# Seven products for eight in the value and gate projections of two of four blocks

## The chip, the cores and the metric

The kernel runs on one core of one Trainium2 chip. The metric is the device time of one execution in microseconds. In the profile PE is TensorE's matmuls, PEld its weight loads, DVE VectorE, ACT ScalarE, POOL GpSimd and SP SyncE, whose queue issues nearly all DMAs.

## The reference

One decoder layer over 2048 tokens of width 1024, in float32: a mixer of two groups of heads, then a squared-ReLU MLP, each between two RMSNorms.

```python
z = h @ w_in                       # h = rmsnorm(x): 2048 x 1024; w_in: 1024 x 3600
gq, gk, gv, gg, glr, hq, hf, hi, hg = jnp.split(z, _split_points(), axis=-1)
log_a = jax.nn.log_sigmoid(glr @ w_gk_up + b_gk) / 16             # GLA, 4 heads, dk 64, dv 128
o_a = chunked_gated_linear_attention(q_a, k_a, v_a, log_a)
o_a = gated_head_norm(o_a, gg, gla_norm_w)                        # rmsnorm(o) * w * silu(gate)
f = lb + (1 - lb) * jax.nn.sigmoid(hf)                            # HGRN2, 4 heads, df 128, dv 128
o_b = chunked_gated_linear_attention(q_b, 1 - f, v_b, jnp.log(f))
o_b = gated_head_norm(o_b, hg, hgrn_norm_w)
mix = jnp.concatenate([o_a, o_b], axis=-1) @ w_out
h = x + rmsnorm(mix, post_mix_norm)
h = h + rmsnorm(jnp.square(jax.nn.relu(rmsnorm(h, pre_mlp_norm) @ w_up)) @ w_down, post_mlp_norm)
```

The change concerns the columns of `w_in` that make the values (`gv`, `hi`) and the gates of the outputs (`gg`, `hg`).

## The kernel before

Every operand is split into a high part, rounded to fp32r, and the rest (`split`: a copy on ACT makes the high part, a subtraction on DVE or POOL the low one). Each product is three matmuls, high x high, high x low, low x high (`mm3`, L301 to L303, which accumulate in PSUM).

The mixer runs over four blocks `b` of 512 tokens. `hn[b]` holds the normalised input, transposed: 8 tiles `act` of 128 channels by 512 tokens, high and low. A block runs four units in the order `u` = 0, 2, 3, 1; units 0 and 1 are pairs of GLA heads, 2 and 3 of HGRN2 heads. A unit has two parts on TensorE:

- `zchan` makes the q, k or f, q channels, 128 channels by 512 tokens, with the weights as TensorE's stationary operand.
- `values` makes 256 value and 256 gate columns, tokens on partitions. For each of 4 token tiles it multiplies 8 input tiles of 128 tokens with 8 weight pieces of 512 columns, 24 matmuls. Unit 0 has 16 more columns (`glr`) and does 272 and 256 columns in two runs of 24. ACT and DVE evict each tile: a copy, and the sigmoid chain for the gate.

Chunk work (scores, states, transposes, outputs) of a unit runs as generator tasks (`spawn`), of which each `step` emits one piece between the products. After the units `out_proj` multiplies the eight heads' outputs with `w_out` in two halves of 512 columns, and beside it `prepare` makes `hn` of the next block. rstd values (`rs`, L310) are one operation on POOL each.

The weights come in 72 pieces a block: per unit 4 or 8 channel pieces and 8 value pieces, then 16 for `out_proj`, always read in this order. Block 0 loads raw pieces (`in_w_mix` to `wr`, 4 buffers, 256 KB), splits them (ACT and POOL, L291 and L292) and stores the parts in the DRAM tensor `w_split` (L126), as block 1 does for its first 12. From there on pieces of 512 KB are loaded from `w_split` (L114) as soon as one of 12 buffers `w` is freed:

```python
if self.split < i or i >= self.freed + self.LIVE:
    return
z = self.part()
y.nc.sync.dma_start(z[:, :, :n].bitcast(F32), self.store[i % PIECES, :, :, :n])
```

A framework schedules the program onto the engines' queues and puts in the semaphores; on SP the DMAs are issued in queue order, one waiting for its buffer holds back those behind it, and each waits for the one eight places ahead to land. After the mixer come `up` and `down` (the MLP), which already use seven half-size products for eight on operands made and stored beforehand. They are not changed. A second, slower layer with `exact` set follows behind a test of the data; it is not executed here.

Of the kernel before, what the change touches and what calls it, by code (L numbers as in the profile page):

```python
# [27 lines left out]
WM = 528  # L28
# [15 lines left out]
def pieces():  # L44


    out = []
# [16 lines left out]
    return out


class Weights:
# [7 lines left out]
    LATE = 12

    def __init__(self, layer, store):
        self.layer, self.plan, self.raw, self.parts = layer, [], {}, {}
        self.store = store
        self.loaded = self.split = self.taken = self.freed = 0  # L80

    def add(self, n, chan=False, eng="vector"):
        self.plan.append((n, chan, eng))

    def part(self):
        y = self.layer
        return y.wp.tile([P, 2, WS], F32R, tag="w", name=y.name("w"), bufs=self.LIVE)

    def give(self, z):

        n, chan, _ = self.plan[self.split]
        hi, lo = z[:, 0, :n], z[:, 1, :n]
        if chan:
            hi, lo = (x.rearrange("p (k n) -> p k n", n=P) for x in (hi, lo))
        self.parts[self.split] = (hi, lo)
        self.split += 1

    def load(self):
        y = self.layer
        while self.loaded < len(self.plan):  # L100
            i = self.loaded
            n = self.plan[i][0]
            if i < PIECES + self.LATE:
                if i >= self.split + self.RAW:
# [4 lines left out]
                self.raw[i] = raw
            else:  # L110
                if self.split < i or i >= self.freed + self.LIVE:
                    return
# [1 line left out]
                y.nc.sync.dma_start(z[:, :, :n].bitcast(F32), self.store[i % PIECES, :, :, :n])  # L114
# [32 lines left out]
class Layer:
# [1405 lines left out]
```

## Time and profile before

| | |
|---|---|
| runs | 2272.88, 2272.98, 2270.74 us, median 2272.88 |
| profiled execution | 2269.14 us, span 2267.3 us, mean granted TensorE clock 0.995 |
| mixer, four blocks | 0 to 985 us: 250 for block 0, 245 for each other |
| up and down | 985 to 2267 us |
| busy over the span | PE 98%, DVE 62%, ACT 48%, POOL 28% |
| DMA | 428.02 MB, mean 189 GB/s |

The busy times of PE are of instructions whose modelled ends overlap, so the length of a matmul in a stream is read from the distance between starts. PEld runs beside PE.

### The profile page before, as it was taken

What the parts mean: (1) busy time and instruction counts of PE and PEld (TensorE: products, weight loads), DVE (VectorE), ACT (ScalarE), POOL (GpSimd) and SP (SyncE); (2) the same over time, 40 slices, a digit from 0 to 9 for tenths busy, and PEclk for the clock granted to TensorE, in tenths of its full rate; (3) what the DMA queues carried; (4) which work ended last, traced back from release to release, by engine and by line L of the source; (5) the groups of instructions that cost most, each with busy time, mean ns of one, the idle gap of its engine ahead of it and who ended that gap; (6) DMA issues with size and microseconds to landing.
All of it is one profiled execution on the core that took longest, in us unless ns stands there. A gap on an engine that the chain in (4) does not pass through costs nothing.

```text
span 2267.3 us, 30672 instructions
## 1 busy us (share of the span) xinstructions
PE 2216.5 (98%) x10922; PEld 1830.8 (81%) x10922; DVE 1408.5 (62%) x2264; ACT 1089.3 (48%) x2104; POOL 643.5 (28%) x444
## 2 busy tenths in 40 slices
PE   8999999999999999999999999999999999999996
PEld 7788888888888978876888888888778878888884
DVE  6764565343652575377765686656536876777687
ACT  6764565334543554365555565555643322333255
POOL 4444301010100220035522343322322332232344
PEclk9999999999999999999999999999999999999998
DMA  7766974467545974378844474443434433443356
GB/s 244 262 232 241 322 257 149 138 237 281 181 151 176 349 286 158 130 270 281 294 151 152 177 238 163 152 153 144 176 126 135 130 123 110 130 140 117 116 148 132
DMA packets 249810, 428.02 MB, mean 189 GB/s; under 512 B 19872, under 2 KB 93872, under 8 KB 249648
## 3 DMA queue, kind: packets, MB, share of 16 engines
q1 hardware_dynamic: 245520, 418.10, 53.6%
q0 software_dynamic: 3552, 6.82, 1.9%
q8 instruction: 88, 1.44, 0.3%
q10 hardware_dynamic: 576, 1.05, 0.1%
q14 instruction: 74, 0.61, 0.1%
HBM read 289.44 MB, written 136.45 MB: 188 GB/s over the span
## 4 chain that ended last, share of the span: by engine, by line
PE 48%; DVE 2%; DMA 2%; ACT 2%; issue 1%; POOL 1%; SPq 0%; DVEq 0%; ACTq 0%; POOLq 0%
PE Y_f L1057 3%; PE Y_f L1059 3%; PE Y_f L1058 3%; PE Y_f L1358 3%; PE Y_f L1359 3%; PE Y_f L1360 3%; PE X_f L1358 2%; PE X_f L1360 2%; PE X_f L1359 2%; PE Z_f L1059 2%; PE Z_f L1057 2%; PE Z_f L1058 2%; PE Z_f L1360 2%; PE Z_f L1359 2%; PE Z_f L1358 2%; PE X_f L1059 2%
## 5 line engine op out<-in xcount | busy, mean ns | idle before, releaser
L301 PE MATMUL zp_f<-w_f,act_f 128*128 128x512 f32 (+2 forms) x896 | 328.6, 367 | 4.2 <-DVE ct_f L319 3.3
L302 PE MATMUL zp_f<-w_f,act_f 128*128 128x512 f32 (+2 forms) x896 | 325.0, 363 | 0.0
L303 PE MATMUL zp_f<-w_f,act_f 128*128 128x512 f32 (+2 forms) x896 | 323.4, 363 | 0.0
L944 ACT ACTIVATE u_f<-raw_f 128x1024 fp32r<-128x1024 f32 x107 | 113.6, 1061 | 331.9 <-PE Y_f L1359 225.4
L310 POOL TENSOR_TENSOR rs_f<-ms_f,c_neghalf 128x1 f32<-128x1 f32 (+1 forms) x80 | 65.1, 820 | 658.0 <-DVE ms_f L308 657.5
L938 POOL TENSOR_TENSOR u_f<-raw_f,u_f 128x1024 fp32r<-128x1024 f32 x49 | 120.4, 2457 | 305.5 <-ACT u_f L944 304.5
L301 PEld LDWEIGHTS zp_f<-w_f,act_f 128*128 128x128 f32 x896 | 168.6, 188 | 31.3 <-DVE ct_f L319 3.7
L303 PEld LDWEIGHTS zp_f<-w_f,act_f 128*128 128x128 f32 x896 | 168.7, 188 | 25.3 <-issue 0.5
L302 PEld LDWEIGHTS zp_f<-w_f,act_f 128*128 128x128 f32 x896 | 168.9, 189 | 24.3 <-issue 0.5
L301 PE MATMUL zp_f<-act_f,w_f 128*128 128x512 f32 x384 | 151.9, 399 | 7.9 <-ACT act_f L294 7.9
L302 PE MATMUL zp_f<-act_f,w_f 128*128 128x512 f32 x384 | 152.3, 397 | 0.1
L303 PE MATMUL zp_f<-act_f,w_f 128*128 128x512 f32 x384 | 151.9, 395 | 0.0
L1313 DVE TENSOR_TENSOR acc_f<-acc_f,Y_f 128x1024 f32<-128x1024 f32 (+1 forms) x91 | 107.5, 1182 | 64.5 <-PE Y_f L1360 63.2
L1358 PE MATMUL Y_f<-act_f,u_f 128*128 128x512 f32 x368 | 142.3, 390 | 4.8 <-ACT Y_f L1350 2.6
L1359 PE MATMUL Y_f<-act_f,u_f 128*128 128x512 f32 x368 | 143.4, 390 | 0.0
L1360 PE MATMUL Y_f<-act_f,u_f 128*128 128x512 f32 x368 | 142.8, 390 | 0.0
L292 POOL TENSOR_TENSOR w_f<-wr_f,w_f 128x512 fp32r<-128x512 f32 (+1 forms) x76 | 105.3, 1395 | 106.1 <-ACT w_f L291 105.4
L944 ACT ACTIVATE w_f<-t_f 128x512 fp32r<-128x512 f32 x128 | 80.1, 629 | 109.7 <-PE Y_f L1058 56.6
L1059 PE MATMUL X_f<-act_f,w_f 128*128 128x512 f32 x256 | 100.2, 391 | 3.6 <-DVE w_f L941 2.7
L1077 DVE TENSOR_TENSOR ev_f<-Y_f,p_f 128x512 f32<-128x512 f32 x94 | 64.6, 688 | 62.8 <-PE Y_f L1059 62.7
L1313 DVE TENSOR_TENSOR acc_f<-acc_f,Z_f 128x1024 f32<-128x1024 f32 (+1 forms) x62 | 73.2, 1181 | 47.6 <-PE Z_f L1360 47.4
L941 DVE TENSOR_TENSOR w_f<-t_f,w_f 128x512 fp32r<-128x512 f32 x96 | 79.9, 832 | 36.7 <-ACT w_f L944 36.7
(294 smaller groups left out, 5767.0 us busy)
## 6 DMA issues: line engine op xcount, KB each, us to landing
w_f<-w_split SPq DMA_DIRECT2D x188, 512.0 KB, 6.3
raw_f<-u_operands SPq DMA_DIRECT2D x224, 256.0 KB, 3.0
u_operands<-ev_f SPq DMA_DIRECT2D x223, 256.0 KB, 2.1
w_split<-w_f SPq DMA_DIRECT2D x64, 512.0 KB, 5.2
wr_f<-in_w_up SPq DMA_DIRECT2D x62, 512.0 KB, 3.5
wide_f<-in_x SPq DMA_DIRECT2D x32, 512.0 KB, 6.9
wr_f<-in_w_mix SPq DMA_DIRECT2D x64, 256.0 KB, 5.0
wr_f<-in_w_down SPq DMA_DIRECT2D x28, 512.0 KB, 4.8
```

What stands on the lines that cost most here:

```text
L301: mm(out, a[0], b[0], start=i == 0, stop=False)
L302: mm(out, a[0], b[1], start=False, stop=False)
L303: mm(out, a[1], b[0], start=False, stop=i == n - 1)
L938: nc.gpsimd.tensor_tensor(out, a, b, op)
L944: self.nc.scalar.activation(hi, raw, AF.Copy)
L1057: mm(z, whi[:, k, :], hi, start=first and k == 0, stop=False, skip_group_check=more)
L1058: mm(z, whi[:, k, :], lo, start=False, stop=False, skip_group_check=more)
L1059: mm(z, wlo[:, k, :], hi, start=False, stop=end, skip_group_check=more)
L1313: nc.vector.tensor_add(a[:, cols], a[:, cols], z[:, cols])
L1358: mm(zx, hi[:, k, tok], whi, start=not loaded and k == 0, stop=False, skip_group_check=loaded)
L1359: mm(zx, hi[:, k, tok], wlo, start=False, stop=False, skip_group_check=loaded)
L1360: mm(zx, lo[:, k, tok], whi, start=False, stop=k == 1, skip_group_check=loaded)
```

## The change

In blocks 2 and 3 `values7` replaces `values`. The block's left operand (512 tokens x 1024 channels) is cut into 2 x 2 parts, tokens by channels, and the weights into 2 x 2, channels by (value, gate). Seven products of 256 tokens x 512 channels x 256 columns, four of them on sums of weight parts and four on sums of left parts, give the four parts of the result (Winograd's form). Each product accumulates two token tiles: for each of 4 channel tiles and 2 token tiles the three matmuls of a split product, 24 in all, of 256 columns (272 in four of unit 0's products, which carry the `glr` columns).

```diff
+    SEVEN = ((0, "base", 0), (4, "sums", 0), (5, "sums", 2), (1, "base", 1), (6, "sums", 1), (2, "base", 2),
+             (3, "sums", 3))
...
+        for step, (i, _, _) in enumerate(self.SEVEN):
+            self.w.pump(2)
...
+            for j in range(2):
+                whi, wlo = self.w.take()
+                for k in (2 * j, 2 * j + 1):
+                    for m in range(2):
+                        hi, lo = left(i, k, m)
...
+                        for a, b in ((hi, whi), (hi, wlo), (lo, whi)):
+                            mm(zm, a, b[:, k % 2, :n], start=opens and k == 0 and b is whi and a is hi,
+                               stop=k == 3 and a is lo, skip_group_check=not opens)
+                self.w.free()
```

Products add into the same banks (X, Y, Z): the result of product 0 is copied to the second bank, and the 512-wide evictions stand between the products. A unit's value pieces in blocks 2 and 3 are 14 of 512 KB, each used by one product for two channel tiles and freed at once, instead of 8 that stay for all token tiles; a block has 96 pieces instead of 72.

The sums of the weights are made once, in block 1, by a task that begins after unit 0 and is drained before `out_proj`. `rows` is the order of pieces, `stage` gives a buffer `st` (3 of them):

```diff
+    def value_sums(self):
...
+        sub = nc.gpsimd.tensor_sub
+        for u in UNITS:
+            w = width(u)
+            for k in range(4):
+                r = []
+                for row in (k, k + 4):
+                    r.append(self.wp.tile([P, WM], F32, tag="wr", name=self.name("wr"), bufs=Weights.RAW))
+                    nc.sync.dma_start(r[-1][:, :2 * w], io["w_mix"][rows["value", u, row * P], :, :2 * w])
+                yield
...
+                sub(t1, g0, v0[:, :256])
+                sub(t3, g, g0)
+                yield
+                sub(t2, g, t1)
+                sub(t4, v[:, :256], t2)
+                yield
+                for half in range(2):
+                    z = self.sum_parts()
...
+                    self.split(hi, lo, raw[:, half * 512:half * 512 + 512].rearrange("p (k n) -> p k n", n=256),
+                               eng=nc.gpsimd)
+                    for t in range(2):
+                        self.keep_sum(u, half * 2 + t, k, z[:, t * 512:t * 512 + 512], 0, 256)
+                    yield
+                if w > 256:
...
@@ mixer
+                if b == 1 and u == 0:
+                    sums = self.spawn(self.value_sums())
+            if b == 1:
+                self.drain(sums)
             self.out_proj(b)
```

`keep_sum` stores 128 x 512 floats (high and low of one sum) to the DRAM tensor `w_sums`. The left operand's sums for blocks 2 and 3 are made in `prepare`, which now takes the input tiles in pairs (k, k + 4); per pair four operations on DVE and two splits (ACT and POOL), kept in `s` and `st` buffers:

```diff
+        nc.vector.tensor_add(a22, a21, a22)
+        nc.vector.tensor_sub(a21, a11, a21)
+        nc.vector.tensor_sub(a11, a22, a11)
+        nc.vector.tensor_sub(a12, a12, a11)
+        hi, lo = self.sum_slot(), self.sum_slot()
+        for h, z in enumerate((x, y)):
+            cols = slice(h * TB, h * TB + TB)
+            self.split(hi[:, cols], lo[:, cols], z, eng=nc.gpsimd)
```

The buffers `w` go from 12 to 8, and 5 buffers `s` come in; block 0 uses these for 16 of its pieces, block 1 for the sums of weights and blocks 2 and 3 for left sums. A stored piece now has the columns in another order (for each 256 columns high, then low).

```diff
-    LIVE = 12
+    BUFS = {"w": 8, "s": 5}
     RAW = 4
```

`out_proj` takes the pieces of half 0 in the outer loop, with four token tiles in four PSUM banks, and evicts half 0 by DVE instead of ACT; half 1 goes two token tiles at a time.

```diff
+        zs = [self.zp() for _ in range(NCH)]
+        for i in range(KT):
...
+            w = self.w.take()
+            for t in range(NCH):
+                part(zs[t], t, w, i)
+                if i == KT - 1:
+                    evac(zs[t], t, 0)
+            self.w.free()
```

On TensorE, in unit 2 of block 2, the first token tile stood so before (`at` is PSUM of the chunk tasks):

```order
L301 MATMUL zp_f957_5691<-w_f913_5425,act_f817_4821 128x512
L302 MATMUL zp_f957_5691<-w_f913_5425,act_f817_4821 128x512
L721 MATMUL at_f949_5634<-c_ident_61,ct_f844_4985 128x128 x4
L303 MATMUL zp_f957_5691<-w_f913_5425,act_f817_4821 128x512
L301 MATMUL zp_f957_5691<-w_f914_5427,act_f820_4840 128x512
L302 MATMUL zp_f957_5691<-w_f914_5427,act_f820_4840 128x512
```

Now there stand the two token tiles of product 0, and, after product 4, product 5 on left sums:

```order
L806 MATMUL zp_f1163_6709<-w_f1121_6504,act_f903_5153 128x256 x6
L806 MATMUL zp_f1163_6709<-w_f1121_6504,act_f910_5193 128x256 x6
L806 MATMUL zp_f1163_6709<-w_f1132_6548,act_f916_5239 128x256 x6
L806 MATMUL zp_f1163_6709<-w_f1132_6548,act_f926_5293 128x256 x6
...
L806 MATMUL zp_f1168_6746<-w_f1134_6564,st_f912_5216 128x256 x2
L806 MATMUL zp_f1168_6746<-w_f1134_6564,st_f913_5217 128x256
```

A piece of weights serves 12 matmuls of half the width, where it served 12 of the full width over four token tiles.

On SP, in block 1, the first pieces of unit 1 stood before in one row, each waiting for a buffer that TensorE frees:

```order
L114 DMA w_f676_3911<-w_split_74 128x2x512 [waits DMAHW0_49,PE_49]
L114 DMA w_f679_3933<-w_split_74 128x2x512 [waits DMAHW1_49,PE_49]
L114 DMA w_f689_3976<-w_split_74 128x2x512 [waits DMAHW2_49,PE_49]
L114 DMA w_f691_3995<-w_split_74 128x2x512 [waits DMAHW3_49,PE_49]
L114 DMA w_f699_4027<-w_split_74 128x2x512 [waits DMAHW4_49,PE_49]
L114 DMA w_f713_4199<-w_split_74 128x2x512 [waits DMAHW5_49,PE_49]
```

Now the task's raw loads and stores stand between them:

```order
L419 DMA wr_f824_4814<-in_w_mix 128x512 [waits DMAHW0_49,Pool_49]
L419 DMA wr_f828_4831<-in_w_mix 128x512 [waits DMAHW1_49,Pool_49]
L459 DMA w_sums_75<-s_f817_4788 128x512 [waits DMAHW2_49,Pool_49]
L459 DMA w_sums_75<-s_f817_4788 128x512 [waits DMAHW3_49]
L459 DMA w_sums_75<-s_f821_4802 128x512 [waits DMAHW4_49,Pool_49]
L459 DMA w_sums_75<-s_f821_4802 128x512 [waits DMAHW5_49]
L139 DMA w_f746_4329<-w_split_74 128x1024 [waits DMAHW6_49,PE_49]
L419 DMA wr_f829_4833<-in_w_mix 128x512 [waits DMAHW7_49,Pool_49]
L139 DMA w_f747_4331<-w_split_74 128x1024 [waits DMAHW0_49,PE_49]
```

The weight loads (L139 after the change) stand behind stores that wait for POOL.

On POOL, in the later units of block 1, rstd rows stood alone before:

```order
L310 TENSOR_TENSOR rs_f694_4013<-ms_f693_4011,c_neghalf_65 128x1 [waits DVE_49,Pool_49]
L310 TENSOR_TENSOR rs_f733_4297<-ms_f732_4295,c_neghalf_65 128x4 [waits DVE_49]
L310 TENSOR_TENSOR rs_f738_4316<-ms_f737_4314,c_neghalf_65 128x4 [waits DVE_49]
L310 TENSOR_TENSOR rs_f785_4639<-ms_f784_4637,c_neghalf_65 128x4 [waits DVE_49,Pool_49]
L310 TENSOR_TENSOR rs_f790_4658<-ms_f789_4656,c_neghalf_65 128x4 [waits DVE_49,Pool_49]
```

Now they stand among the task's subtractions (L424 to L428, and L319 of `split`):

```order
L424 TENSOR_TENSOR st_f835_4854<-wr_f833_4850 128x256 [waits DMAHW3_49]
L337 TENSOR_TENSOR rs_f770_4441<-ms_f769_4439,c_neghalf_65 128x4 [waits DVE_49]
L337 TENSOR_TENSOR rs_f775_4460<-ms_f774_4458,c_neghalf_65 128x4 [waits DVE_49]
L425 TENSOR_TENSOR st_f835_4854<-wr_f834_4852,wr_f833_4850 128x256 [waits DMAHW4_49]
L427 TENSOR_TENSOR st_f835_4854<-wr_f834_4852,st_f835_4854 128x256 [waits Pool_49]
L424 TENSOR_TENSOR st_f840_4873<-wr_f838_4869 128x256 [waits DMAHW5_49]
L428 TENSOR_TENSOR st_f835_4854<-wr_f834_4852,st_f835_4854 128x256 [waits Pool_49]
L319 TENSOR_TENSOR s_f836_4859<-st_f835_4854,s_f836_4859 128x2x256 [waits DMAHW6_49,DMAHW1_49,Activation_49]
```

The rstd rows of unit 3's heads (L337 now) are moved behind subtractions that wait for raw loads and for stores of earlier sums.

More of the change, by code (lines that the diff above doesn't have):

```diff
@@ L27 @@
 NG = FF // P // GF
-WM = 528
+WM = 544
 WS = 576
@@ L49, in chan @@
     def chan(*cols):
-        out.extend(("chan", half * 512, [(col, P)]) for half in range(2) for col in cols)
+        out.extend(("chan", u, half * 512, [(col, P)]) for half in range(2) for col in cols)
     for u in UNITS:
@@ L67 @@
 class Weights:
-    LIVE = 12
+    BUFS = {"w": 8, "s": 5}
     RAW = 4
[L75 to L96, printed above, removed]
+    def __init__(self, layer):
+        self.layer, self.plan, self.pending, self.parts = layer, [], [], {}
+        self.loaded = self.taken = self.freed = 0
+        self.live = {"w": 0, "s": 0}
+    def room(self, i):
+        tag = self.plan[i].tag
+        return self.live[tag] < self.BUFS[tag]
@@ L136, in take @@
     def take(self):
-        if self.split == self.taken:
-            assert self.split - self.freed < self.LIVE
+        self.load()
+        while self.taken not in self.parts:
             self.prep()
@@ L143, in free @@
     def free(self, n=1):
-        self.freed += n
+        for _ in range(n):
+            self.live[self.plan[self.freed].tag] -= 1
+            self.freed += 1
 class Layer:
@@ new lines, in sum_parts, with keep_sum @@
+    def sum_parts(self):
+        return self.wp.tile([P, D], F32R, tag="s", name=self.name("s"), bufs=Weights.BUFS["s"])
+    def keep_sum(self, u, which, k, z, col, n):
+        w = width(u) if which > 1 else 256
+        at = self.wparts["sums"][u, which, k // 2, :, k % 2 * 2 * w:k % 2 * 2 * w + 2 * w]
+        if n == w:
+            self.nc.sync.dma_start(at, z.bitcast(F32))
+        else:
+            self.nc.sync.dma_start(at.rearrange("p (a n) -> p a n", a=2)[:, :, col:col + n],
+                                   z.bitcast(F32).rearrange("p (a n) -> p a n", a=2))
@@ L333, in mixer @@
     def mixer(self):
-        for tag, n, width in (("wr", Weights.RAW, WM), ("w", Weights.LIVE, 2 * WS), ("pad", 1, 48)):
-            self.wp.tile([P, width], F32R if tag == "w" else F32, tag=tag, name=self.name(tag), bufs=n)
+        for tag, n, cols in (("wr", Weights.RAW, WM), ("w", Weights.BUFS["w"], 2 * WS), ("s", Weights.BUFS["s"], D),
+                             ("pad", 1, 48)):
+            self.wp.tile([P, cols], F32R if tag in ("w", "s") else F32, tag=tag, name=self.name(tag), bufs=n)
@@ new lines, in out_proj @@
+            w = self.w.take()
[4 more added lines that the diff above has]
+            self.w.free()
+            self.step()
+            if i in (1, 4):
+                self.step()
+        n = 2 if b + 1 < NBLK else 1
+        w = []
+        for t0 in range(0, NCH, n):
+            zs = [self.zp() for _ in range(n)]
+            for i in range(KT):
+                if i % (4 // n) == 0:
+                    self.w.pump(2)
+                if t0 == 0:
+                    w.append(self.w.take())
+                for t in range(n):
+                    part(zs[t], t0 + t, w[i], i)
+                if t0 + n == NCH:
+                    self.w.free()
+                if i * n % 4 == 3 or i * n % 4 == 2 and n == 2:
+                    self.step()
+            for t in range(n):
+                evac(zs[t], t0 + t, 1)
@@ L1478, in build @@
         c["verdict"] = cp.tile([1, 1], I32, name="c_verdict")
-        wsplit = dp.tile([PIECES, P, 2, WM], F32, name="w_split")
+        wd = {"split": dp.tile([PIECES, P, 2 * WM], F32, name="w_split"),
+              "sums": dp.tile([len(UNITS), 4, 2, P, 2 * WM], F32, name="w_sums")}
         h2d = dp.tile([D, T], F32, name="h2_scratch")
```

345 lines of the change are left out of this document (249 added, 96 removed).

## The prediction

> **What bounds the kernel now.** I read the page's busy shares first, then the busy time of each engine by block, then TensorE's waits.
>
> ```profile
> span 2267.3 us, 30672 instructions
> PE 2216.5 (98%) x10922; PEld 1830.8 (81%) x10922; DVE 1408.5 (62%) x2264; ACT 1089.3 (48%) x2104; POOL 643.5 (28%) x444
> ```
> ```profile
> 250.00:495.00 245.00, 245.00 (x1386) 205.03 (x1386) 124.32 (x325) 115.66 (x290) 23.66 (x24) 1.00 0.62 213
> 495.00:740.00 245.00, 245.00 (x1386) 205.03 (x1386) 117.28 (x320) 111.58 (x282) 16.48 (x20) 1.00 0.59 201
> 740.00:985.00 245.00, 245.00 (x1383) 204.72 (x1382) 129.41 (x318) 118.10 (x292) 38.08 (x34) 1.00 0.66 233
> ```
> The three windows are mixer blocks 1, 2 and 3 (columns: stretch, length, PE, PEld, DVE, ACT, POOL, granted clock, DMA share, GB/s). TensorE is busy for all of each 245.0 us at a granted clock of 1.00; the two longest waits of the run lie in block 0:
>
> ```profile
> PE zp_f L301 <- ACT act_f L294: 7.9, 1, 7.9
> PE zp_f L301 <- DVE ct_f L319: 3.3, 1, 3.3
> ```
> So a block's time is the sum of its matmuls, and matmuls taken out are worth their spacing as long as weights arrive. The spacing is the distance of starts, since the durations overlap:
>
> ```profile
> 876.10 0.39 PE L301 MATMUL zp_f<-w_f,act_f 128*128 128x512 f32 x1
> ...
> 892.19 0.40 PE L303 MATMUL zp_f<-w_f,act_f 128*128 128x512 f32 x1
> ```
> ```profile
> 519.69 0.28 PE L302 MATMUL zp_f<-w_f,act_f 128*128 128x256 f32 x1
> ...
> 522.28 0.28 PE L303 MATMUL zp_f<-w_f,act_f 128*128 128x256 f32 x1
> ...
> 522.66 0.28 PE L303 MATMUL zp_f<-w_f,act_f 128*128 128x272 f32 x1
> ...
> 525.29 0.29 PE L303 MATMUL zp_f<-w_f,act_f 128*128 128x272 f32 x1
> ```
> 16.09 us over 71 gaps is 0.2266 us at 512 columns, 2.59 over 22 is 0.1177 at 256, 2.63 over 21 is 0.1252 at 272.
>
> **Blocks 2 and 3: products.** Per block, units 2, 3 and 1 each lose 96 matmuls of 512 columns (21.75 us) and unit 0 loses 96 of 272 and 96 of 256 (23.32 us). Each unit gains 168 half-width ones: 19.77 us, or for unit 0, where four of seven products keep 272 columns, 96 x 0.1252 + 72 x 0.1177 = 20.49 us. That saves 1.98 us in three units and 2.83 in one, 8.77 a block and **17.5 us** in both. The halved width leaves more weight loads in the same time:
>
> ```profile
> L302 PEld LDWEIGHTS zp_f<-w_f,act_f 128*128 128x128 f32 x62 | 11.7, 188 | 0.0
> ```
> A load takes 188 ns, yet the 256-wide rows, with a load for each matmul, run at 117.7 ns: loads overlap there, so I price them at nothing. The other bound is that spacing becomes 188 ns, a rival below. [...]
>
> **Blocks 2 and 3: other engines.** A unit's evictions were four of ACT's 256-wide copies and sigmoid chains per token tile; they become 512-wide.
>
> ```profile
> L538 ACT ACTIVATE wide_f<-zp_f 128x256 f32<-128x256 f32 x60 | 22.8, 380 | 97.0 <-PE zp_f L303 95.3 <-issue 1.5
> L317 ACT ACTIVATE wide_f<-wide_f 128x256 f32<-128x256 f32 x64 | 26.8, 418 | 1.2
> L786 ACT ACTIVATE ct_f<-zp_f 128x512 f32<-128x512 f32 x32 | 19.0, 596 | 0.0
> L291 ACT ACTIVATE w_f<-wr_f 128x512 fp32r<-128x512 f32 x68 | 41.9, 629 | 45.4 <-DMA wr_f<-in_w_mix 30.5 <-POOL w_f L292 8.3 <-issue 5.0
> L547 DVE TENSOR_TENSOR wide_f<-zp_f,wide_f 128x256 f32<-128x256 f32 x60 | 25.4, 423 | 18.6 <-ACT wide_f L320 18.3
> ```
> ACT goes from about 4 x (2 x 0.38 + 3 x 0.418) = 8.1 us to 5 x 0.596 + 8 x 0.629 = 8.0 us a unit, within 20 us of products: nothing. The token sums of the left operand (prepare) add per block 16 DVE operations of 0.42 (6.8 us), 8 ACT copies of 0.63 (5.0) and 8 POOL subtractions of 1.36 (10.9), beside the output projection of the block before:
>
> ```profile
> 476.00:505.00 29.00, 29.00 (x133) 24.15 (x132) 15.00 (x26) 13.91 (x32) 2.98 (x3) 1.00 0.80 287
> 505.00:567.00 62.00, 62.00 (x378) 54.84 (x377) 26.02 (x63) 29.57 (x61) 3.30 (x5) 1.00 0.81 287
> 750.00:812.00 62.00, 62.00 (x378) 54.79 (x378) 32.99 (x62) 35.27 (x71) 14.29 (x13) 1.00 1.00 355
> ```
> In the first window DVE would stand at 21.8, ACT at 18.9 and POOL at 13.9 of 29 us, and the products that read them (4, 5, 6, 2) stand behind unit 0's channel products, 48 x 0.2266 = 10.9 us: nothing. Moving half 0's eviction from ACT to DVE is off the path too. Weights are not free: a unit loads 14 pieces of 512 KB instead of 8, one for 12 matmuls, 1.41 us. The third window (start of block 3) already moves 355 GB/s at DMA share 1.00, where a piece takes 1.48 us. Eight buffers are 11 us of stock. Bounds for both blocks' starts and streaming: 0, and 10 us (two units at 1.48 for 1.41 and a late first piece in each block); I take **1.2**, near the low end, because the saturated window is one unit of four.
>
> **Block 1: the task.** Per unit and row pair it issues on SP 2 loads and 4 stores of 262 KB, on POOL 4 subtractions of 256 columns and 2 of 512, on ACT 2 copies.
>
> ```profile
> L938 POOL TENSOR_TENSOR u_f<-raw_f,u_f 128x1024 fp32r<-128x1024 f32 x49 | 120.4, 2457 | 305.5 <-ACT u_f L944 304.5 <-DMA raw_f<-u_operands 0.7
> L292 POOL TENSOR_TENSOR w_f<-wr_f,w_f 128x512 fp32r<-128x512 f32 x68 | 92.0, 1363 | 101.9 <-ACT w_f L291 101.4 <-PE zp_f L301 0.2
> L938 POOL TENSOR_TENSOR act_f<-ct_f,act_f 128x512 fp32r<-128x512 f32 x1 | 2.4, 2359 | 1.4 <-ACT act_f L944 1.4
> L310 POOL TENSOR_TENSOR rs_f<-ms_f,c_neghalf 128x4 f32<-128x4 f32 x32 | 32.3, 1010 | 473.4 <-DVE ms_f L308 473.1
> 297.00:453.00 156.00, 156.00 (x878) 127.87 (x877) 82.93 (x244) 76.22 (x195) 8.19 (x10) 1.00 0.52 177
> DMA packets 15190, 27.57 MB, mean 177 GB/s; under 512 B 866, under 2 KB 2914, under 8 KB 15178
> ```
> From 1.363 at 512 and 2.457 at 1024 a 256-wide subtraction is estimated at 0.82 us, so a step takes POOL 4 x 0.82 + 2 x 1.363 = 6.0 us, 16 steps 96 us, and ACT 32 x 0.63 = 20 us. The last two rows are the stretch from unit 0's end to the output projection: 156 us in which POOL works 8.2, ACT 76.2 and DVE 82.9. Unit 0's 16 extra columns add 3 small operations in 4 steps, 12 us at the rstd row's 1.0. With those and the 8.2 POOL would be busy 116 of 156. DMA moves 27.6 MB there; 25.2 more make 52.8, or 338 GB/s, 95% of the 355 above. So it fits, at small margin. Matmuls of block 1 don't read the sums; what can reach them is SP's queue, in which a store that waits for POOL stands ahead of the next weight load, and the heads' rstd behind subtractions on POOL (1.0 us each; I take **0.7** for those, bounds 0 and 6, one step).
>
> **Block 1: eight buffers for twelve.** A unit's values hold all eight pieces until its last token tile. Before, the next unit's first pieces came in four spare buffers:
>
> ```profile
> SPq L114 <- PE zp_f L303: 376.3, 103, 23.4
> w_f<-w_split SPq DMA_DIRECT2D x50, 512.0 KB, 5.9
> DMA to landing us min/median/max: 3.5/6.5/10.0
> ```
> SP stood ready and waited 376 us for TensorE to free buffers. Now the first one comes free, in unit 0, after 3 of the last 24 matmuls, 21 x 0.1177 = 2.5 us before the end (0.8 us of transposes follow), and in the others 21 x 0.2266 = 4.8 us. The load needs 3.5 to 10.0 us. Unit 0 to 2: 0.2 to 6.7, I take **1.5**, since the queue is short there. Unit 2 to 3: 0 to 5.2, **0.4**. Unit 3 to 1 and 1 to output projection: 0 to 5.2 each, plus up to eight 262 KB transfers in flight (5.9 us at 355 GB/s); **2.0** and **1.5**, nearer the median landing (6.5 - 4.8 = 1.7). Later pieces are used at 2.7 us each and catch up. Block 0 has 13 buffers for 12: nothing, bounds -1 and 1.
>
> **Sum.** -17.5 + 1.2 + 0.7 + 1.5 + 0.4 + 2.0 + 1.5 = -10.2. The profiled execution took 2269.1 (span 2267.3 and 1.8 around it), so it would take 2258.9; the median of the runs, 2272.9, lies 3.8 above it, and gives **2262.7**.
>
> **Rivals.** (1) Full gain: the next unit's loads land in time after all, stalls below 3 us; 2255 to 2258. For it: the block-1 window's DMA share of 0.52, and the minimum landing of 3.5. Against: the order of SP's queue.
> (2) Queue backlog: three of the boundaries in block 1 meet a queue full of stores (3 to 5.9 us each) and streaming costs 2 to 4, together 11 to 21.7; 2266 to 2277. For it: 338 of 355 GB/s.
> (3) The other side, POOL's pace: the task must be drained before block 1's output projection, so at p us a step TensorE, through SP's stores, waits 16p + 20 - 156. From p = 8.5 it costs; with the other terms it ends above 2277.4 from 9.4. At 10 it gives 24 us: 2287. For it: the single 2.359 row beside 1.363, and DVE's 82.9 busy us; if each of six operations first waits out one DVE operation of 0.42 to 0.7, p is 8.5 to 10.2. Against: the means over 49 and 68 are taken beside a busy DVE too. [...]
> (4) Weight loads of 188 ns set the spacing: 168 x 0.188 = 31.6 us a unit, 9.8 more than before and 79 in eight: about 2358. Against: the 22 gaps of 117.7 ns. [...]
>
> **Chances.** Forecast (stalls 3 to 11, 2258 to 2266) 0.50, full gain 0.18, backlog 0.18, POOL's pace 0.12, weight loads 0.02. 0.2% of 2272.9 is 4.5 us, about what runs of this kernel can tell from nothing: faster is below 2268.3, slower above 2277.4. Faster takes the first two and a quarter of the third, 0.72; slower the last two, 0.14; same the rest, 0.14. The range, 2254 to 2277, holds the first three; the forecast alone 2258 to 2266.
>
> **What the profile after would show.** Right: blocks 2 and 3 about 236 us long each with half-width matmuls at 0.118 and no idle; in block 1, POOL about 116 us busy between unit 0 and the output projection, steps of 6 us, and TensorE idle for 1 to 2 us at the starts of units, released by weight DMAs. Wrong: a gap of 10 us or more ahead of block 1's output projection, with 256-wide POOL subtractions well over 1.1 us (rival 3); spacing above 0.13 (rival 4); waits for weights spread through blocks 2 and 3 (the streaming term was too small); or idle time at block starts behind the left sums, which I priced at nothing.

## The result and the profile after

The changed kernel takes 2290.07 us (median of 4 runs, 2285.14 to 2294.07), the kernel before 2271.81 in the same comparison: a ratio of 1.008, 95% interval 1.0059 to 1.0101. It is slower by 18 us; 2262.7 was forecast, in a range that ended at 2277. The profiled execution took 2285.14. From the page of the changed kernel, and its windows by block, cut at the first matmul of each block (columns as before: PE, PEld, DVE, ACT, POOL, clock, DMA share, GB/s):

```profile
span 2283.3 us, 31913 instructions
PE 2214.2 (97%) x11306; PEld 1848.4 (81%) x11306; DVE 1466.4 (64%) x2294; ACT 1105.3 (48%) x2092; POOL 772.2 (34%) x572
```
```profile
259.60:519.70 260.10, 251.08 (x1387) 208.05 (x1386) 156.07 (x333) 129.15 (x323) 127.15 (x140) 0.99 0.84 299
519.70:758.40 238.70, 237.69 (x1579) 209.65 (x1578) 133.13 (x332) 117.37 (x265) 29.16 (x27) 1.00 0.76 261
758.40:1008.50 250.10, 242.66 (x1570) 213.14 (x1570) 138.08 (x316) 115.66 (x265) 49.42 (x42) 0.98 0.80 280
```
Cut in the same way, the kernel before took 245.2, 245.3 and 244.1 us for these blocks. So block 2 gains 6.6 us, block 1 loses 14.9 and block 3 loses 6.0: the sum, 14.3, is nearly all of the 16.0 us between the spans. In block 2 TensorE is idle for 1.0 us, in block 1 for 9.0 and in block 3 for 7.4. The waits of TensorE in three stretches, block 1's unit 0 (255 to 300 us), the end of unit 3 and the start of unit 1 in block 1 (400 to 460), block 3's first 90 us (758 to 850):

```profile
PE zp_f L329 <- POOL w_f L319: 2.9, 2, 1.6
```
```profile
PE at_f L1003 <- DVE ct_f L947: 2.1, 1, 2.1
PE zp_f L328 <- DMA w_f<-w_split: 1.7, 1, 1.7
PE at_f L993 <- DVE ct_f L948: 1.2, 1, 1.2
```
```profile
PE zp_f L806 <- DVE ct_f L346: 3.6, 1, 3.6
PE at_f L1154 <- DVE wide_f L1148: 2.2, 1, 2.2
PE zp_f L806 <- ACT zp_f L812: 1.1, 1, 1.1
```
Most of them are waits for VectorE or POOL; only 1.7 us in these stretches are for a weight load. The half-width matmuls themselves run as forecast, here 24 of product 0 in unit 3 of block 2 and what follows them:

```profile
642.37 3.04 PE L806 MATMUL zp_f<-w_f,act_f 128*128 128x256 f32 x24
645.24 0.60 PE L1003 MATMUL at_f<-c_ident,ct_f 128*128 128x128 f32 x4
```
2.87 us from start to start for 24 is 0.1196 us each, against 0.1177: 1.3 us more over a block's 672, and no sign of the 0.188 of the weight loads.

**The granted clock.** A wait costs more than itself. The first row is a window of block 1 with the POOL waits, the second of block 3 behind the 3.6 us; the other three cut block 3's start, where the wait of 2.2 us ends at 771.73, into pieces of 3.41 us:

```profile
270.70:281.00 10.30, 7.30 (x44) 6.66 (x43) 2.96 (x2) 5.36 (x10) 8.82 (x8) 0.83 0.99 350
826.00:833.00 7.00, 7.00 (x76) 6.66 (x74) 6.97 (x22) 5.17 (x12) 0.00 (x0) 0.76 1.05 345
768.27:771.68 3.41, 1.21 (x6) 0.67 (x4) 2.96 (x7) 3.21 (x9) 2.53 (x4) 1.00 0.98 272
771.68:775.09 3.41, 3.36 (x15) 3.36 (x16) 3.31 (x2) 0.58 (x2) 3.41 (x4) 0.50 1.05 417
775.09:778.50 3.41, 3.41 (x30) 3.41 (x29) 2.71 (x5) 2.31 (x5) 3.07 (x3) 1.00 0.81 321
```
In the second TensorE is busy throughout, at 0.76 of its clock. The last three show what this mean is made of: after 3.41 us with 2.20 us of idle time the clock is at half for the next 3.41 us. Block 1 has two such stretches, block 3 three; each costs about 1.7 us. With them block 3 adds up: 244.1 before, less the 7.5 us that the products save (8.77 less 1.3), plus 7.4 of idle time and 5.1 of slow clock, is 249.1 of the 250.1 measured. In block 1, 9.0 of idle time and 3.4 of slow clock leave 2.5 of the 14.9 us unexplained.

### The profile page after: what moved, and what is told of

Read it like the earlier page. It is cut to its first block, busy times and chain, and to the rows that moved or that the text cites. A ratio compares the mean times of both kernels' runs of the same rounds, so it can differ in the third digit from the quotient of the medians.

```text
span 2283.3 us, 31913 instructions
## 1 busy us (share of the span) xinstructions
PE 2214.2 (97%) x11306; PEld 1848.4 (81%) x11306; DVE 1466.4 (64%) x2294; ACT 1105.3 (48%) x2092; POOL 772.2 (34%) x572
## 4 chain that ended last, share of the span: by engine, by line
PE 47%; DMA 2%; DVE 2%; issue 1%; ACT 1%; POOL 1%; SPq 0%; DVEq 0%; ACTq 0%; POOLq 0%
PE Y_f L1338 3%; PE Y_f L1340 3%; PE Y_f L1339 3%; PE Y_f L1639 3%; PE Y_f L1640 3%; PE Y_f L1641 3%; PE X_f L1639 2%; PE X_f L1641 2%; PE X_f L1640 2%; PE Z_f L1639 2%; PE Z_f L1640 2%; PE Z_f L1641 2%; PE X_f L1339 2%; PE X_f L1340 2%; PE X_f L1338 2%; PE Z_f L1340 2%
## 5 line engine op out<-in xcount | busy, mean ns | idle before, releaser
L337 POOL TENSOR_TENSOR rs_f<-ms_f,c_neghalf 128x1 f32<-128x1 f32 (+1 forms) x80 | 64.9, 820 | 473.7 <-DVE ms_f L335 473.5
L329 PE MATMUL zp_f<-w_f,act_f 128*128 128x512 f32 (+2 forms) x548 | 202.8, 371 | 3.0 <-POOL w_f L319 2.9
L328 PE MATMUL zp_f<-w_f,act_f 128*128 128x512 f32 (+2 forms) x548 | 203.3, 375 | 1.1 <-ACT ct_f L723 1.1
L330 PE MATMUL zp_f<-w_f,act_f 128*128 128x512 f32 (+2 forms) x548 | 200.7, 369 | 0.0
L328 PE MATMUL zp_f<-act_f,w_f 128*128 128x512 f32 x328 | 130.6, 398 | 2.5 <-DMA w_f<-w_split 2.5
L330 PE MATMUL zp_f<-act_f,w_f 128*128 128x512 f32 x328 | 129.9, 396 | 0.0
L329 PE MATMUL zp_f<-act_f,w_f 128*128 128x512 f32 x328 | 129.0, 393 | 0.0
L329 PEld LDWEIGHTS zp_f<-w_f,act_f 128*128 128x128 f32 x548 | 104.4, 191 | 19.7 <-POOL w_f L319 3.6
L328 PEld LDWEIGHTS zp_f<-w_f,act_f 128*128 128x128 f32 x548 | 103.5, 190 | 19.0 <-issue 1.4
L330 PEld LDWEIGHTS zp_f<-w_f,act_f 128*128 128x128 f32 x548 | 104.2, 190 | 16.7 <-issue 0.3
L319 POOL TENSOR_TENSOR w_f<-wr_f,w_f 128x512 fp32r<-128x512 f32 (+1 forms) x59 | 84.7, 1450 | 74.1 <-ACT w_f L318 63.4
L1219 POOL TENSOR_TENSOR ev_f<-ev_f,ev_f 128x512 f32<-128x512 f32 x40 | 63.0, 1575 | 124.3 <-ACT ev_f L1362 64.1
```

Source lines behind the costliest of these rows:

```text
L328: mm(out, a[0], b[0], start=i == 0, stop=False)
L329: mm(out, a[0], b[1], start=False, stop=False)
L330: mm(out, a[1], b[0], start=False, stop=i == n - 1)
L1219: nc.gpsimd.tensor_tensor(out, a, b, op)
```

## The experiments

Times of a block or unit are between the first channel matmuls (zchan) in the profiled execution; "rest of block 1" is from unit 2 to the end of the block. Each ratio is to runs of the kernel before in the same comparison (medians 2270.8 to 2271.8). The unchanged down stage took 615 to 622 us from its first to its last matmul in these executions, so the spans of single ones say less than the blocks. Blocks vary too where their code is the same: block 1 by 3 us (e9 and e11), its rest by 4 us (e13 and e14, of which 12.5 and 3.4 us stood at half clock), block 3 from 246.6 to 250.5 (the changed kernel, e1, e2, e3, e5, e6). So a difference of a few us in one block counts only where the medians bear it out.

| | median us | ratio to before (95%) | block 1 | rest of block 1 | block 2 | block 3 |
|---|---|---|---|---|---|---|
| before | 2271.8 | | 245.2 | 208.4 | 245.3 | 244.1 |
| after | 2290.1 | 1.0059-1.0101 | 260.1 | 216.4 | 238.7 | 250.1 |
| e1 odd pieces on DVE | 2289.3 | 1.0064-1.0100 | 261.9 | 217.9 | 238.0 | 250.5 |
| e2 buffers s in unit 0 | 2284.5 | 1.0047-1.0073 | 257.0 | 215.0 | 238.7 | 248.9 |
| e3 no task | 2277.8 | 1.0021-1.0041 | 251.8 | 208.4 | 237.9 | 250.4 |
| e4 no left sums in block 3 | 2285.0 | 1.0048-1.0079 | 261.6 | 217.0 | 238.4 | 247.0 |
| e5 task without arithmetic | 2281.0 | 1.0026-1.0053 | 257.0 | 211.1 | 238.2 | 246.6 |
| e6 task without stores | 2288.7 | 1.0063-1.0090 | 258.7 | 216.3 | 239.3 | 247.5 |
| e7 late combine | 2278.5 | 1.0022-1.0044 | 260.3 | 216.7 | 238.1 | 242.0 |
| e8 seven products in block 2 only | 2291.2 | 1.0075-1.0102 | 261.6 | 217.0 | 238.9 | 251.0 |
| e9 = e2 + e7 | 2277.1 | 1.0018-1.0041 | 258.2 | 214.9 | 238.5 | 239.0 |
| e10 = e9, task on DVE | 2273.2 | 0.9997-1.0017 | 254.8 | 211.5 | 238.5 | 239.9 |
| e11 = e9, left sums on DVE | 2274.0 | 0.9999-1.0017 | 261.3 | 217.6 | 237.3 | 238.4 |
| e12 before with 8 buffers | 2298.1 | 1.0106-1.0139 | 248.2 | 208.1 | 251.2 | 250.6 |
| e13 = all mends | 2269.4 | 0.9976-0.9995 | 256.7 | 214.5 | 237.3 | 238.3 |
| e13 without the task | 2262.3 | 0.9940-0.9966 | 248.0 | 208.1 | 237.3 | 239.5 |
| e14 = e13 + e1 | 2269.6 | 0.9980-0.9997 | 251.9 | 210.5 | 237.3 | 237.6 |

**e1 and e2: unit 0 of block 1.** From its first value matmul to unit 2's first channel matmul it took 32.5 us, 25.6 before (the two texts say 33.1 and 25.8).

```diff
-                    if b == 0 and i < self.LATE and i % 2 and kind == "value":          # e1
+                    if i < self.LATE and i % 2 and kind == "value":
-                if b == 0 and (i < 4 or 12 <= i < 16 or 16 < i < 56 and i % 3 == 2):    # e2
+                if b == 1 and i < 4 or b == 0 and (i < 4 or 12 <= i < 16 or ...):
```


> The changed kernel, but the odd ones of unit 0's eight value pieces in block 1 are split by DVE again, as before the change (there all eight are split by POOL). Theory POOL-splits: unit 0's values in block 1, which took 33.1 us against 25.8 before, return to 26 to 27.5 us and the whole gains 5 to 7 us (2290 to about 2284). Theory eight-buffers: the pieces are late because only 8 buffers w are there; values stay above 31.5 us and the whole within 2 us of 2290.

> The changed kernel, but unit 0's four channel pieces in block 1 go to buffers s (free at that time), so that all eight w are free for its value pieces. Theory eight-buffers: unit 0's values in block 1 fall from 33.1 to below 28 us, the whole gains 4 to 7 us. Theory POOL-splits: the pieces are still split one after the other on POOL; values stay above 31 us and the whole within 2 us of 2290.

e1 changed nothing (32.8 us): who splits does not matter. In e2 both waits for POOL's `w_f` are gone, and the last value matmul stands 26 us after the first, as before the change. So the pieces could not be split ahead while eight `w` also held the channels' pieces. But unit 0 as a whole only went from 43.7 to 41.9 us (30.7 from the first value matmul to unit 2, in place of the "below 28" of the expectation), and the whole's gain of 5.6 us isn't clear of noise, since the intervals overlap: low-rank matmuls of the gate, which stood inside unit 2, now stand ahead of it and wait. Timeline of TensorE in e2, and its windows there:

```profile
299.42 0.73 PE L328 MATMUL at_f<-ct_f,wgk_f 16*128 16x512 f32 x2 [1.06 <-ACT ct_f L318]
...
302.54 0.63 PE L330 MATMUL zp_f<-act_f,w_f 128*128 128x512 f32 x1
302.97 0.63 PE L328 MATMUL zp_f<-act_f,w_f 128*128 128x512 f32 x1
```
```profile
299.07:302.48 3.41, 3.06 (x11) 2.00 (x12) 2.18 (x4) 2.54 (x6) 0.37 (x2) 1.00 1.02 360
302.48:305.89 3.41, 3.41 (x9) 2.65 (x8) 0.69 (x1) 0.43 (x1) 0.00 (x0) 0.50 1.03 423
```
3 us after a wait of 1.06 us the spacing of 512-wide matmuls is 0.43 us, about twice the 0.2266, for 3.41 us. The 3.41 us ahead hold only 0.35 us of idle time, and the six low-rank matmuls (16*128, where the others are 128*128); whether these have a part in it no run shows. In e10 TensorE is idle for 1.06 us in 297 to 359 us too, and the clock stayed at 1.00 there; in e13, with a wait of 1.1 us on the same operation, 302.1 to 320 us stand at 0.84.

**e3, e5, e6: the task, its DMAs, its arithmetic.** e3 drops the spawn and drain; e5 stores the raw tiles; e6 returns from `keep_sum` at once.

```diff
-                    self.split(hi, lo, raw[...], eng=nc.gpsimd)                          # e5, and the four sub()
-                        self.keep_sum(u, half * 2 + t, k, z[:, t * 512:t * 512 + 512], 0, 256)
+                        self.keep_sum(u, half * 2 + t, k, r[half][:, :512], 0, 256)
```


> The changed kernel without the task in block 1: no sums of weights are made, and blocks 2 and 3 load pieces of the same size from w_split in their place (the value products are computed with these). Theory queue-and-POOL (the task's loads, stores and subtractions delay the weight loads and the other engines): block 1 from unit 2 to its end falls from 216.4 us to 208 to 210 (before: 208.4), the whole gains 6 to 9 us. Theory eight-buffers: the boundaries wait for freed buffers whether the task runs or not; 213 to 217 us, the whole gains under 3.

> The changed kernel, but the task in block 1 leaves out its arithmetic: it loads the raw pieces and stores them as they are in the places of the sums (same DMAs, nothing on POOL, ACT or DVE). Theory lock (POOL's subtractions hold up VectorE's operations with two SBUF inputs, VectorE falls behind and TensorE waits for it): block 1 from unit 2 to its end falls from 216.4 us to 208 to 210.5, as without the task (208.4). Theory queue (the stores and loads stand ahead of weight loads on SP and take DMA time): it stays at 213 to 217.

> The changed kernel, but the task makes the sums and doesn't store them (its raw loads stay; blocks 2 and 3 load pieces of the same size from w_split in their place). Theory lock: block 1 from unit 2 to its end stays at 213 to 217 us, with TensorE waiting for VectorE near the end of unit 3. Theory queue: with 64 stores of 256 KB gone from SP's queue it falls to 208 to 210.5 us, and no wait of TensorE on w_split is left.

Without the task the rest of block 1 takes 208.4 us, exactly as before: eight buffers cost nothing at those three boundaries. The DMAs alone (e5) cost 2.7 us, between its two expectations, and 1.7 of them are slow clock behind the waits ahead of unit 2 (TensorE is idle for none of the 211.1 us). The arithmetic with its raw loads (e6) costs 7.9, all together 8.0. The medians agree: leaving out the arithmetic gains 9.1 us, leaving out the stores 1.4. So it is the arithmetic. Yet POOL is not late by its own pace; its operations in the changed kernel (255 to 520 us):

```profile
L319 POOL TENSOR_TENSOR s_f<-st_f,s_f 128x512 fp32r<-128x512 f32 x32 | 42.4, 1331 | 13.2 <-ACT s_f L318 10.7 <-DMA w_f<-w_split 2.2
L425 POOL TENSOR_TENSOR st_f<-wr_f,wr_f 128x256 f32<-128x256 f32 x16 | 13.5, 847 | 9.4 <-DMA wr_f<-in_w_mix 9.4
L427 POOL TENSOR_TENSOR st_f<-wr_f,st_f 128x256 f32<-128x256 f32 x16 | 13.0, 812 | 0.0
L424 POOL TENSOR_TENSOR st_f<-wr_f 128x256 f32<-128x256 f32 x16 | 12.8, 801 | 8.9 <-DMA wr_f<-in_w_mix 8.9
L428 POOL TENSOR_TENSOR st_f<-wr_f,st_f 128x256 f32<-128x256 f32 x16 | 12.5, 779 | 0.4
```
A step is 0.847 + 0.812 + 0.801 + 0.779 + 2 x 1.331 = 5.9 us, as priced (6.0). VectorE is slowed. Its scans in the log decay, in 303 to 440 us of the kernel before, of the changed one, and of e5:

```profile
L643 DVE TENSOR_TENSOR_SCAN ct_f<-c_ones,ct_f 128x128 f32<-128x128 f32 x24 | 8.3, 405 | 0.1
```
```profile
L925 DVE TENSOR_TENSOR_SCAN ct_f<-c_ones,ct_f 128x128 f32<-128x128 f32 x21 | 12.1, 629 | 0.0
```
```profile
L906 DVE TENSOR_TENSOR_SCAN ct_f<-c_ones,ct_f 128x128 f32<-128x128 f32 x24 | 8.3, 406 | 0.1
```
The same instruction takes 405 ns, 629 beside POOL's subtractions, 406 when these are left out (with the task's copies on ACT) and the DMAs stay. Not every operation is stretched; in the changed kernel, the first with both operands in SBUF, the second with one in PSUM (`zp`):

```profile
L948 DVE TENSOR_TENSOR ct_f<-ct_f,ct_f 128x512 f32<-128x512 f32 x5 | 4.8, 968 | 0.0
L346 DVE SCALAR_TENSOR_TENSOR ct_f<-zp_f,ct_f 128x512 f32<-128x512 f32 x8 | 5.3, 677 | 0.4 <-ACT ct_f L345 0.4
```
Before they took 682 and 678 ns. One operation with a single operand in SBUF was stretched too (564 ns for 424). All of VectorE in those 137 us, for e3 and the changed kernel:

```profile
303.00:440.00 137.00, 136.83 (x758) 112.31 (x759) 78.77 (x233) 68.99 (x176) 8.34 (x11) 1.00 0.54 188
```
```profile
303.00:440.00 137.00, 132.77 (x727) 108.66 (x728) 93.53 (x221) 76.14 (x196) 70.01 (x86) 0.99 0.83 296
```
78.8 us of work become 93.5 with fewer instructions. In the changed kernel 3.3 of the 5.1 us that TensorE is idle in the rest of block 1 are waits for VectorE. e6 shows a second path: its longest wait is 3.5 us for `w_split`, at 423.8, without a single store in the queue. There the raw loads, which wait for POOL to free `wr`, stand ahead of the weight loads on SP:

```profile
396.49 23.14 SPq L420 DMA_DIRECT2D wr_f<-in_w_mix  x8
419.69 1.37 SPq L139 DMA_DIRECT2D w_f<-w_split  x3
```
That expectation's "no wait on w_split" fell with the queue theory, and "waiting for VectorE" held for 1.4 us only.

**e4, e7, e8: block 3.**

```diff
-        later = x if b > 1 else None                                                     # e4, e8
+        later = x if b == 2 else None
-                self.spawn(self.combine(0, halves))
             for u in UNITS:
+                if u == 3 and b == NBLK - 1:                                             # e7
+                    self.spawn(self.combine(0, halves))
```


> The changed kernel without the left operand's sums of block 3 (four products there use tiles of the input unsummed): 16 DVE operations, 8 ACT copies and 8 POOL subtractions less beside the output projection of block 2; products, weights and DMA of block 3 stay. Theory left-sums (DVE and POOL, which also build the MLP's first operands there, fall behind): block 3 falls from 250.1 us to 239 to 242 and the whole gains 8 to 11 us. Theory DMA (the 24 pieces more saturate the queue in block 3's first 90 us): block 3 stays above 247 us, the whole within 3 us of 2290.

> The changed kernel, but in block 3 the task that makes the MLP's first left operands (combine: loads of 256 KB, 16 POOL operations, 28 stores) is spawned ahead of unit 3 instead of at the block's start. Theory crowding (block 3's first 90 us hold the left sums, 24 pieces more and this task; POOL and the queue are late and VectorE is held up): the stall of 3.7 us ahead of unit 2's values and the wait at the block's start go, block 3 falls from 250.1 to 238 to 243 us and the whole gains 6 to 12 us. Theory late glr (unit 0's low-rank columns are complete only with the last of seven products, and the gate chain stands ahead of unit 2's sigmoids on ACT and DVE): the 3.7 us stay, block 3 stays above 247.

> The changed kernel with seven products in block 2 alone; block 3 does eight on pieces of w_split, without left sums (buffers, the output projection's order and the task in block 1 stay). Theory seven-in-3 (block 3's loss comes with its pieces, sums and late glr): block 3 returns to 243 to 246 us, and the whole gains 4 to 7 us on 2290. Theory common parts (eight buffers, evictions on DVE): block 3 stays at 249 or more with eight products more of time, 255 or above, and the whole loses.

`combine` is a task of the kernel before, unchanged, which makes operands of the MLP at the start of block 3 (POOL additions L1189 to L1200). With the left sums' subtractions it keeps POOL busy for all of 758 to 769 us. VectorE's operations there read (and below them POOL's subtractions of 755 to 775 us):

```profile
759.27 2.31 DVE L1141 SCALAR_TENSOR_TENSOR wide_f<-wide_f,rs_f,post_f 128x1024 f32<-128x1024 f32 x1 [1.70 <-POOL rs_f L337]
761.50 1.51 DVE L597 TENSOR_TENSOR ct_f<-ct_f,ct_f 128x256 f32<-128x256 f32 x1
762.93 1.51 DVE L595 TENSOR_TENSOR ct_f<-ct_f,ct_f 128x256 f32<-128x256 f32 x1
```
```profile
L319 POOL TENSOR_TENSOR s_f<-ct_f,s_f 128x512 fp32r<-128x512 f32 x4 | 8.2, 2059 | 0.0
```
The first takes 1.27 us in the kernel before at block 3's start (`752.14 1.27`), the others 0.42 where POOL is quiet (e11). Here POOL is slowed as well, 2.06 us for what took 1.33 in the task. TensorE waits there for L1148, behind them. The larger stall, 3.6 us ahead of unit 2's values, is a chain of the gate of unit 0 standing ahead of unit 2's sigmoid on VectorE; timeline of DVE, and of PE with the low-rank matmuls that start this chain:

```profile
821.73 2.40 DVE L925 TENSOR_TENSOR_SCAN ct_f<-c_ones,ct_f 128x128 f32<-128x128 f32 x4
...
824.92 0.69 DVE L346 SCALAR_TENSOR_TENSOR ct_f<-zp_f,ct_f 128x512 f32<-128x512 f32 x1
```
```profile
815.98 0.73 PE L328 MATMUL at_f<-ct_f,wgk_f 16*128 16x512 f32 x2
...
825.66 4.50 PE L806 MATMUL zp_f<-w_f,act_f 128*128 128x256 f32 x23 [3.56 <-DVE ct_f L346]
```
With `combine` moved (e7) both waits go, block 3 takes 242.0 us and the whole 11.6 less. In e7 the low-rank matmuls stand elsewhere too:

```profile
808.09 0.73 PE L328 MATMUL at_f<-ct_f,wgk_f 16*128 16x512 f32 x2
```
Unit 2 begins at 795.66 in the changed kernel and at 792.38 in e7, so they come 20.3 and 15.7 us into it: behind 83 of its 96 channel matmuls and behind 61 (34 in the kernel before; in block 2 of the changed kernel, which has no such wait, 61). In the changed kernel and in e1 to e6, which have seven products and `combine` at the block's start, they stand behind 83; in e7, e9, e10, e11 and e13 behind 61. So e7 doesn't tell crowding on POOL from this order, and the theory of the late low-rank columns had hold of the larger wait, though it expected it to stay.

Without left sums (e4) the wait at the block's start goes: unit 0 takes 34.2 us there, 35.9 to 37.2 in the six executions with the same block 3. The larger stays at 3.6, and block 3 as a whole, 247.0, is not outside what those six show. e4's expectation, either all or nothing, missed. Since unit 0 takes 34.4 us in e7, with left sums and without `combine`, the 2 to 3 us at the block's start come from the two together.

In e8 eight products in block 3 bring 251.0 instead of 243 to 246: the 3.6 us stall is gone, but units 0 and 2 together take 106.2 us (99.2 before), with waits for weights and for the gate's low-rank products between them. So neither theory held as put. Eight pieces held in 8 buffers are a possible reason, which e8 does not show by itself.

**e9, e10, e11: the mends.**

```diff
-        sub = nc.gpsimd.tensor_sub                                                       # e10, in value_sums
+        sub = nc.vector.tensor_sub
-            self.split(hi[:, cols], lo[:, cols], z, eng=nc.gpsimd)                       # e11, in sums_of
+            self.split(hi[:, cols], lo[:, cols], z)
```


> The changed kernel with two of the mends at once: unit 0's channel pieces of block 1 in buffers s, and combine spawned ahead of unit 3 in block 3. Theory (eight buffers in block 1's unit 0, crowding in block 3, both independent): the gains of the single runs add up, 2290 - 5.6 - 11.6 = 2273, 2270 to 2277; block 1 about 257 us, block 3 about 242. Rival (a wait moved away returns later, since POOL still makes block 1's end late and the queue is no shorter): 2278 or more.

> As the last one, but the task's four 256-wide subtractions per step run on DVE instead of POOL (64 x 0.42 = 27 us more on DVE, 52 less on POOL). [...] Rival VectorE-bound (it is busy 93.5 of 137 us there already): no gain, or up to 8 us lost.

> As e9, but the low parts of the left operand's sums (8 subtractions of 512 a block) are made on DVE instead of POOL. Theory lock: at the starts of blocks 2 and 3 DVE's operations return to their lengths (0.42 for 256-wide ones, which took 1.51 us at block 3's start), block 3 and 2 gain 1 to 3 us each. Rival: with combine gone from there POOL no longer holds them up; within 1.5 us of e9.

e9 stands between its two expectations (2277.1), though block 3 fell to 239.0: e2's gain did not add up in block 1. In e10 the whole gains 3.9 us on e9, where the rival had no gain, and the intervals don't overlap; the rest of block 1 falls from 214.9 to 211.5, and scans from 560 to 449 ns. But this doesn't settle how. VectorE's own 64 subtractions take 0.52 to 0.66 us each, and its busy time in 303 to 440 us rises from 88.0 to 103.2. What TensorE no longer waits for are weights; its waits in the rest of block 1, in e9 and in e10:

```profile
PE zp_f L328 <- DMA w_f<-w_split: 3.8, 2, 3.4
```
```profile
PE zp_f L328 <- DMA w_f<-w_split: 0.6, 1, 0.6
```
So e10 fits the second path, raw loads that no longer wait for POOL, at least as well as a VectorE that POOL slows less. e11 brings all VectorE operations of block 3's start back (1.29 and 0.42 us, against 1.92 and up to 0.79 in e9; its rows for the 1024-wide one and a 256-wide one):

```profile
L1142 DVE SCALAR_TENSOR_TENSOR wide_f<-wide_f,rs_f,post_f 128x1024 f32<-128x1024 f32 x3 | 3.9, 1286 | 0.6 <-POOL rs_f L337 0.4
...
L596 DVE TENSOR_TENSOR ct_f<-ct_f,ct_f 128x256 f32<-128x256 f32 x4 | 1.7, 418 | 0.0
```
Block 2 gains 1.2 us on e9 and block 3 0.6, at the low end of the theory or below it; the whole median moved 3.1, more than these explain.

**e12: eight buffers by themselves.**

```diff
-    LIVE = 12
+    LIVE = 8
```


> The kernel before with 8 weight buffers instead of 12 and nothing else changed. Theory eight-buffers: unit 0's values in block 1 grow from 25.8 us to 31 to 34, as in the changed kernel, and in blocks 2 and 3 by 2 to 7 us (pieces needed within 6 us of each other, loaded at 1.4 us each); the other boundaries lose under 1 us; the whole 2280 to 2293. Rival (the loss in block 1's unit 0 came with the paired input tiles, the evictions on DVE or the queue of the new order): within 4 us of 2271.

26 us slower, more than expected, and not in the place expected: unit 0's values in block 1 took 27.5. Waits of TensorE in its blocks 1 to 3:

```profile
PE zp_f L301 <- DMA w_f<-w_split: 7.2, 3, 5.0
PE zp_f L301 <- ACT wide_f L317: 3.0, 1, 3.0
```
The 5.0 us are at block 3's start. By the code the old output projection holds eight pieces until its last token tile, where the new order frees each piece of half 0 after its use; that this is what makes eight buffers bearable in the changed kernel is likely, but no run has the new order taken back.

**e13, e14: all mends.**

> All four mends: buffers s for unit 0's channel pieces in block 1, combine ahead of unit 3 in block 3, the task's subtractions and the low parts of the left sums on DVE. Theory (independent parts): 2273.2 - 3 = 2270, 2267 to 2273; blocks 1, 2 and 3 about 255, 237.5 and 238.5 us. Rival (DVE full): 2275 or more.

> As e13_all without the task: no sums of weights are made, blocks 2 and 3 load pieces of the same size from w_split in their place. Theory task: what is left in block 1 is the task's; block 1 falls to 245 to 248 us and the whole to 2259 to 2264. Rival other parts (eight buffers and the new order): block 1 stays at 250 or more, the whole above 2265.

> As e13_all, with the odd ones of unit 0's value pieces in block 1 split by DVE, as before the change. Theory POOL-splits (they matter once buffers are free): block 1 gains 1 to 3 us on e13_all. Rival: within 1 us, as in the run that had this alone.

Blocks 1, 2 and 3 of e13:

```profile
259.90:516.60 256.70, 252.60 (x1388) 209.60 (x1387) 169.42 (x408) 131.43 (x321) 72.37 (x65) 0.97 0.84 295
516.60:753.90 237.30, 237.30 (x1580) 209.54 (x1579) 132.66 (x339) 113.44 (x259) 17.20 (x20) 1.00 0.76 259
753.90:992.20 238.30, 237.70 (x1570) 208.60 (x1569) 133.73 (x321) 120.28 (x270) 37.42 (x35) 1.00 0.84 298
```
2269.4 us beats the changed kernel by 20.7 and the kernel before by 0.15% (ratio 0.9985, 0.9976 to 0.9995), the smallest of differences. Blocks 2 and 3 now have TensorE busy for all but 0.6 us and gain 8.0 and 5.8. The same without the task is 7.1 us faster, as expected of the task, and takes 248.0 in block 1, 2.8 more than before. How much of e13's 256.7 is the task's can't be read from the block: e14, equal to e13 in its median as its rival said, took 251.9 in block 1, with 3.4 us at half clock instead of 13.7.

## Why the prediction was wrong

By blocks the sum said +6.1 us for block 1 and -8.2 each for blocks 2 and 3, -10.2 in all. The profiled execution shows +14.9, -6.6 and +6.0. So of the 26 us between -10.2 and the +16.0 of the spans, 14 lie in block 3, 9 in block 1 and 2 in block 2; the rest is outside the mixer. The steps that failed are the left sums and the gate chain of block 3, both at nothing, and in block 1 the refill of unit 0 at nothing and the task at 0.7.

- **Products** (-17.5): right. Spacing 0.1196 for 0.1177; block 2 gains 6.6 us in the changed kernel and 8.0 in e13, where 8.77 less the 1.3 of spacing were due.
- **Weight loads at nothing**, against rival 4's spacing of 188 ns: right; the half-width matmuls stand 119.6 ns apart with a load of 192 ns for each (PEld, 642 to 660 us).
- **Streaming** (1.2): right; one wait for `w_sums`, 1.0 us in block 2.
- **Block 3 beside `combine`**, the largest miss. Two things were at nothing. The left sums: busy shares (21.8, 18.9 and 13.9 of 29 us) were added as if the engines were independent, and the window was the one ahead of block 2; at block 3's start `combine`, which the prediction never named, already runs on POOL. Together they lengthen VectorE's operations from 0.42 to 1.51 us and POOL's from 1.33 to 2.06, and cost 2 to 3 us of unit 0, slow clock included; moved apart (e7) or with the sums left out (e4) they don't. That idle time behind the left sums was among the prediction's own signs of being wrong. The gate chain of unit 0: no term had it. Its low-rank columns are complete only with the last of seven products, its matmuls stood 20.3 us into unit 2, and TensorE waited 3.6 us, with two stretches of slow clock in the 14 us behind. With `combine` moved block 3 took 242.0 and 239.0 us, with the subtractions moved too 238.4.
- **Block 1's unit 0**: the boundary ahead of it was left out. Eight buffers kept its pieces from being split ahead, 6.9 us from its first value matmul to its end; e2 shows the two waits go, but only 1.8 us of the unit come back.
- **Block 1's other boundaries** (1.5 + 0.4 + 2.0 + 1.5 = 5.4): too large, since without the task they cost 0.0; with it TensorE waited 2.5 us for weights (0.7 and 1.7).
- **The task**: priced at 0.7 beside the boundaries; it cost 8.0 (e3), nearly all by its arithmetic (e5, e6). That the sum for this stretch, 6.1, came near 8.0 is luck: both its parts were off. Rival 3 had POOL and VectorE in each other's way, but put the price on POOL's pace: p stayed at 5.9, far from the 8.5 at which it was to begin, and VectorE was slowed. Its scan went from 405 to 629 ns and a 512-wide operation with both operands in SBUF from 682 to 968, while one with an operand in PSUM stayed at 678 and 677; by what mechanism no run shows.
- **The clock**: no term had it, 3.4 us in block 1 and 5.1 in block 3.
- What stays open: how block 1's 8 us divide between VectorE's lateness (3.3 us of waits in the changed kernel, 0.4 in e9) and the weight loads behind raw loads that wait for POOL (2.5 and 3.8); whether the larger wait of block 3 would go by the order of the low-rank matmuls alone; and why e12 loses in other places than e2 and the changed kernel.

## What to carry to other kernels

Work put on an idle POOL is not free where VectorE is on a chain that TensorE waits for: look at the length of VectorE's operations with both inputs in SBUF beside POOL's (here 682 ns became 968), not at busy shares, and at which loads wait for a buffer that POOL frees. When a task is added, list every task that already runs in that stretch, the unchanged ones too, and every boundary at which a smaller buffer set must be refilled. And count a short stall of TensorE with its slow clock behind it: here 1.7 us more for each stretch of 3.41 us at half clock.

## What the hardware showed that was not expected

In the changed kernel the granted clock fell to half for eight stretches of 3.41 us (0.50 in 771.68 to 775.09 us, 1.00 on both sides), in the kernel before for two, and in both once more at the end of the span. In these two profiled executions, past the first 11 us, each of the twelve falls came behind 3.41 us with 1.6 us of idle time of TensorE or more (2.20 ahead of 771.68); stretches with up to 1.9 us of idle time also went without a fall. In e2 one came behind 0.35 us and six low-rank matmuls of 16 rows. So about the same wait can cost 1.7 us more in one execution than in another. And VectorE's scan with one operand of constants is stretched like a two-tensor operation (405 to 629 ns). Which engine is stretched differs: POOL's own subtractions hardly are in the task (1.331 us, 1.363 over the kernel before), but clearly at block 3's start (2.059).
